# A decoder layer on one core: the first k tile for eight column groups in place of two k tiles for four, and six matmuls of a constant block around the norm factor

## The chip, the core and the metric

The kernel runs on one core of a Trainium2 chip. The core has engines that each work through their own list of instructions: TensorE (PE, matrix products; PEld is its loading of stationary operands), VectorE (DVE) and ScalarE (ACT) for elementwise work, GpSimd (POOL) and SyncE (SP), which here only issues loads. The engines run beside one another and wait for each other through semaphores. PE writes to an accumulation memory called PSUM; everything else lives in the on-chip memory SBUF, to which DMA brings the data.

The metric is the device time in microseconds. Before the change it is 1531.68 us, the median of three runs (1531.55 to 1531.72).

## What is computed

One decoder layer with 256 tokens of width 2048, in float32. Cut to what matters here:

```
mod = silu(c) W_ada + b_ada -> shift1, scale1, gate1, shift2, scale2, gate2
h   = RMSNorm(x)(1+scale1)+shift1
p   = h W_in, columns split into [retention q,k,v,g | HGRN2 q,f,i,g | branch gate A | branch gate B]
yA, yB = two attention-like branches on p, each with its own output product
x   = x + gate1 * ( (sigmoid(gA)*yA + sigmoid(gB)*yB) W_out )
h2  = RMSNorm(x)(1+scale2)+shift2
x   = x + gate2 * ( (silu(a) * b) W_down ),   [a, b] = split(conv3(h2 W_up))
out = RMSNorm_final(x)
```

The change touches the first half of the third line: 12 column groups of W_in, 512 columns each, that hold the q, f, i of the one branch and the q, k, v of the other (6144 of the columns).

## The kernel before

**Three products for one.** Each float32 factor is split into a high and a low half of a shorter type. A product is high x high, high x low and low x high. For a weight tile ACT makes the high half (line 165, tile `wh`), and DVE subtracts it from the raw tile to make the low half, here called the rest (line 170, `wl`). `load` (line 156) brings the raw tile by SP's queue; it has 12 buffers, `wh` and `wl` 4 each.

**Groups and k tiles.** The 2048 rows of W_in are 16 k tiles of 128. One k tile of one column group is 256 KB, and here called a unit: 192 units in all. For 8 of the 12 groups the result is kept transposed (`mm_cols`, lines 200 to 202: 12 matmuls a unit on 256 columns), for 4 (numbers 4, 5, 10 and 11) in rows (`mm_rows`, lines 187 to 189: 6 matmuls on 512).

**h arrives k tile by k tile.** For k tile k, scale and shift come from dot products over `w_ada`, which DVE takes in halves of 512 KB (`ada_dot`, line 389: four such halves for one k tile). ACT adds up the halves (lines 400, 401, 403) and makes the modulated tile's high half `hT` (line 336) and a full copy `h` (line 338 or 340); DVE makes its low half (line 341). So a k tile costs DVE four halves of about 1.1 us and a few small instructions, and a group can only go as far in k as h has come.

**The norm factor.** `token_rstd` sums the squares over the partitions by matmuls with a column of ones (line 289), ACT takes the root (line 298), DVE the reciprocal (line 299), and four matmul records with an identity (line 303) spread it over the partitions into PSUM as `rx`. `times` (line 379) multiplies x by it, and only then can hT for k tile 0 be made.

**Where sums are kept.** PSUM has two `pg` tiles of two banks each and four `po` tiles of one. Groups 0 and 1 (RESIDENT) keep their four `po` tiles from the first k tile to the last. Every other group is summed in a `pg` tile for as many k tiles as h has, and then leaves: at its first visit ACT copies the sum to SBUF (`take`, line 700), at later visits DVE adds it to what is there (line 702).

**The start.** FIRST = 4: for k tile 0 and then k tile 1, groups 0 to 3 run (lines 711 to 730). Groups 2 and 3 hold a `pg` tile each through both k tiles, and are copied out behind the loop (line 739). Everything up to line 733 that is marked with `pin` stays in program order on its engine; a scheduler places the rest at build time. The finished order of each engine is fixed in the program.

**The loop behind it.** From line 743 on `work` counts the units done. `have = min(KT, 2 + int((work - LAG) / ADA_EVERY))` with ADA_EVERY = 11 and LAG = 1 says how many k tiles of h there are to use. Groups are visited in turn 0 to 11, and each visit runs the group's k tiles up to `have` (two at a time in `pieces`). Between the pieces `pump` runs background generators by credit: the dot products of later k tiles, and the branches' work once their groups are complete. After these 192 units come the other products of the layer, in the same manner, up to the end.

Of the kernel before, what the change touches and what calls it, by code (L numbers as in the profile page):

```python
# [14 lines left out]
BF16 = mybir.dt.bfloat16  # L15
I32 = mybir.dt.int32
AF = mybir.ActivationFunctionType
ALU = mybir.AluOpType

P = 128  # L20
# [9 lines left out]
G = 512  # L30
NORM_EPS = 1e-6
HEAD_EPS = 1e-5
FIRST = 4
RESIDENT = 2
ADA_EVERY = 11
LAG = 1
NOSYNC = mybir.DependencyInfo(mybir.DependencyClass.NoSync, mybir.DependencyReason.DATA)
SMALL = 70

# [16 lines left out]
class Kernel:  # L56
# [172 lines left out]
    def constants(self):  # L229
        nc, a, c = self.nc, self.a, self.consts  # L230
        self.ones = c.tile([P, P], F32, name="ones")
        nc.vector.memset(self.ones, 1.0)
        self.eps1 = c.tile([P, 1], F32, name="eps1")
        nc.vector.memset(self.eps1, NORM_EPS)
        self.eps2 = c.tile([P, 1], F32, name="eps2")
        nc.vector.memset(self.eps2, HEAD_EPS)
        self.halfpi = c.tile([P, 1], F32, name="halfpi")
        nc.vector.memset(self.halfpi, math.pi / 2)

        self.silu = []  # L240
        self.sc = c.tile([P, D + 1], F32, name="sc")
        nc.vector.memset(self.sc[:, D:], 1.0)
        rows = [self.blk([1, GW], name="crow") for _ in range(2)]
        for u, row in enumerate(rows):
            nc.scalar.dma_start(out=row, in_=a["c"][:, u * GW : (u + 1) * GW])
        self.small_loads(nc.scalar, ("ident", "gn1"))
        for u in range(4):
            at = slice(u * G, (u + 1) * G)
            ps = self.po()
            nc.tensor.matmul(ps, lhsT=self.ones[0:1, :], rhs=rows[u // 2][:, u % 2 * G : (u % 2 + 1) * G], start=True, stop=True)  # L250
            self.silu.append((self.sc[:, at], ps))

    def small_loads(self, engine, names):
        for name in names:
            ap = self.a[name]
            t = self.consts.tile(list(ap.shape), ap.dtype, name=name)
            self.tc.keep_in_program_order(engine.dma_start(out=t, in_=ap))
            setattr(self, name, t)
# [22 lines left out]
    def token_rstd(self, parts):  # L281


        nc = self.nc
        ps = self.po()[:, :NT]
        for i, z in enumerate(parts):
            for t in range(NT):

                nc.tensor.matmul(
                    ps[:, t : t + 1],  # L290
                    lhsT=z[:, t * P : (t + 1) * P],
                    rhs=self.ones[:, 0:1],
                    start=i == t == 0,
                    stop=i == len(parts) - 1,
                    skip_group_check=True,
                )
        q = self.small([P, NT], name="rq")
        nc.scalar.activation(q, ps, AF.Sqrt, bias=self.eps1, scale=1.0 / D)
        self.pin(nc.vector.reciprocal(q, q))

        ps = self.po()[:, :T]
        for t in range(NT):
            nc.tensor.matmul(ps[:, t * P : (t + 1) * P], lhsT=q[:, t : t + 1].to_broadcast([P, P]), rhs=self.ident, start=True, stop=True)
        return ps

    def sqrt_table(self):
# [359 lines left out]
    def run(self):  # L666
        nc, a = self.nc, self.a
# [11 lines left out]
        def act(k):  # L679
            return hT[k // 2][:, k % 2, :]  # L680

        def ada1(k):
            if k > 0 and k % 2 == 0:
                ins = self.times(k, 2, rx_sb)
                self.tc.add_manual_dep(ins.ins, self.last.ins.name, NOSYNC, reason="behind the weights traced ahead of it")
            yield from self.scale_shift("ada1", k, s1, t1, self.gn1)
            if k % 2 == 0:
                hT[k // 2] = self.blk([P, 2, 2 * T], F32R, name="hT")
            self.modulated(act(k), self.xT[k // 4][:, k % 4, :], k, s1, t1)
            yield 0.7  # L690

        accs = [self.blk([P, NT, G] if c0 in ROWS else [P, 4, T], name="p") for c0 in ATT]
        done = [0] * len(ATT)
        mms = [self.mm_rows if c0 in ROWS else self.mm_cols for c0 in ATT]

        def take(g, ps, fresh):
            for at, z in self.parts(ps, ATT[g] in ROWS):
                dst = accs[g][:, at, :]
                if fresh:
                    nc.scalar.activation(dst, z, AF.Copy)  # L700
                else:
                    nc.vector.tensor_tensor(dst, dst, z, ALU.add)


        ada = [ada1(k) for k in range(KT)]
        for _ in range(3):
            next(ada[0])
        rx = self.token_rstd(parts)
        rx_sb = c.tile([P, T], F32, name="rx_sb")
        ps = [self.po2(), self.po2(), self.pg(), self.pg()][:FIRST]  # L710
        for k in range(2):
            for i in range(4 if k else 1):
                if k and i == 1:
                    self.times(k, 1, rx)
                next(ada[k])
            if k == 0:
                self.times(k, 1, rx)

            ahead = 2 * k
            uppers = [self.upper(a["wa"][g][:, k : k + 1, :], 1, G) for g in range(ahead + 1)]  # L720
            rests = [self.rest(z) for z in uppers[:ahead]]
            for _ in ada[k]:
                pass
            for g in range(FIRST):
                if g >= ahead:
                    rests.append(self.rest(uppers[g] if g < len(uppers) else self.upper(a["wa"][g][:, k : k + 1, :], 1, G)))
                wh, wl = rests[g]
                if k == g == 0:
                    self.pin(nc.scalar.activation(rx_sb, rx, AF.Copy))
                mms[g](ps[g], act(k), wh[:, 0, :], wl[:, 0, :], k == 0, k == 1 and g >= RESIDENT)  # L730
        for _ in range(2):
            next(ada[2])
        self.ordered = False
        for gen in ada[2:]:
            self.start(gen, 1)
        for g in range(FIRST):
            done[g] = 2
            if g >= RESIDENT:
                take(g, ps[g], True)
        self.pace(1, 4, ADA_EVERY / 2)  # L740
        self.pace(0, 3.5, 24)

        work = 2 * FIRST
        g = FIRST
        att, gates = [], []
        small = False
        while min(done) < KT:
            if work > SMALL and not small:
# [3 lines left out]
                self.start(self.lower_bound())  # L752
            have = min(KT, 2 + int((work - LAG) / ADA_EVERY))
            m = have - done[g]
# [18 lines left out]
            g = (g + 1) % len(ATT)  # L773
            if have == KT and done[0] < KT:
                g = min(i for i in range(len(ATT)) if done[i] < KT)
# [9 lines left out]
        for j in range(4):  # L785
            ps = self.rows(a["wb"][j], act)
# [55 lines left out]
        for j in range(4):  # L842
            last = j == 3
            x1.append(self.load_rows(j))
            g = self.row(self.gate["gate1"], j, "g1")
            ps = self.products(self.mm_rows, self.po2() if last else self.pg(), a["wout"][j], actm, 0, KT, hold=4 * last)
# [14 lines left out]
            if j == 2:  # L861
                part = self.row_part(ss)
# [232 lines left out]
```

## Time and profile before

| | before |
|---|---|
| median of 3 runs | 1531.68 us (1531.55 to 1531.72) |
| the profiled execution | 1532.02 us |
| its span, first to last instruction | 1529.9 us |
| PE busy | 1511.9 us, 99% |
| DVE busy | 1178.0 us, 77% |
| ACT busy | 841.5 us, 55% |
| 16 DMA engines, main queue | 76.1% |

The span is what the profile's rows cover; the execution's own time is 2.1 us more. Busy shares are means over the span. A row of the timeline gives start, duration, engine, source line, operation, output <- inputs, shape and count, and in brackets the idle time before and what ended it. `PE ... <- ACT hT L336` means that PE waited for line 336's result on ACT. A matmul's duration runs to the modelled end of its flow through the array, so the next starts before the last has ended: the space between starts, not the duration, is what a matmul costs PE.

### The profile page before, as it was taken

To read this page: it belongs to the slowest core of one execution; us is meant where nothing else is said; L and a number is where in the kernel's file an instruction comes from. 1 tells how busy PE (TensorE), PEld (TensorE's weight loads), DVE (VectorE), ACT (ScalarE), POOL (GpSimd) and SP (SyncE) were. 2 spreads that over 40 slices of the span, in tenths; PEclk is the share of its full clock that TensorE was granted. 3 is DMA by queue.
4 is the path that set the end of the run, shared out by engine and by line. 5 is a ranking of instruction groups with operands and counts; after the bars stand their busy time and mean duration, and the time that the engine had idled before them with its cause. 6 is when DMAs were issued, how large, how long until landed. Compare 5 with 4: busy or idle time off the path is not lost.

```text
span 1529.9 us, 22149 instructions
## 1 busy us (share of the span) xinstructions
PE 1511.9 (99%) x8258; PEld 1304.4 (85%) x8258; DVE 1178.0 (77%) x1610; ACT 841.5 (55%) x1194; POOL 4.0 (0%) x8
## 2 busy tenths in 40 slices
PE   8999999999999999999999999999999999999997
PEld 6999999888888888888878888888888888888886
DVE  7899996997998977898767777777777769455454
ACT  6655455766865554445456565555556558344343
POOL 0000000000000000000000000000000000000000
PEclk9999999999999999999999999999999999999999
DMA  9999996777777789989947777777777766676651
GB/s 375 370 355 328 311 332 217 240 278 239 274 240 264 256 293 323 323 300 341 336 126 231 231 235 233 237 227 232 232 231 232 227 191 192 204 209 206 194 166 55
DMA packets 110992, 385.68 MB, mean 252 GB/s; under 512 B 12802, under 2 KB 13346, under 8 KB 110884
## 3 DMA queue, kind: packets, MB, share of 16 engines
q1 hardware_dynamic: 110016, 383.14, 76.1%
q8 instruction: 64, 1.05, 0.3%
q10 hardware_dynamic: 868, 1.13, 0.2%
q14 instruction: 44, 0.36, 0.1%
HBM read 382.11 MB, written 2.11 MB: 251 GB/s over the span
## 4 chain that ended last, share of the span: by engine, by line
PE 95%; ACT 2%; DVE 1%; DMA 1%; issue 0%; SPq 0%; DVEq 0%; ACTq 0%
PE pg L187 13%; PE pg L188 13%; PE pg L189 13%; PE po L935 11%; PE pg L935 10%; PE po L937 5%; PE pg L937 5%; PE po L189 3%; PE po L187 3%; PE po L188 3%; PE pg L202 3%; PE pg L200 3%; PE pg L201 3%; PE po L565 1%; PE po L200 1%; PE po L201 1%
## 5 line engine op out<-in xcount | busy, mean ns | idle before, releaser
L170 DVE TENSOR_TENSOR wl<-raw,wh 128x1024 fp32r<-128x1024 f32 (+1 forms) x536 | 635.2, 1190 | 286.6 <-ACT wh L165 282.4
L165 ACT ACTIVATE wh<-raw 128x1024 fp32r<-128x1024 f32 (+1 forms) x536 | 551.1, 1033 | 544.1 <-PE pg L189 189.0
L389 DVE SCALAR_TENSOR_TENSOR raw<-raw,sc 128x1024 f32<-128x1024 f32 x192 | 233.5, 1219 | 0.0
L935 PE MATMUL pg<-h2T,wh 128*128 128x512 f32 x704 | 221.6, 396 | 0.6 <-ACT h L371 0.6
L935 PE MATMUL po<-h2T,wh 128*128 128x512 f32 x704 | 221.1, 395 | 0.0
L187 PE MATMUL pg<-wh,hT 128*128 128x512 f32 x512 | 202.7, 396 | 0.2 <-ACT p L700 0.2
L188 PE MATMUL pg<-wl,hT 128*128 128x512 f32 x512 | 200.1, 391 | 0.7 <-DVE wl L170 0.7
L189 PE MATMUL pg<-wh,hT 128*128 128x512 f32 x512 | 199.8, 390 | 0.0
L937 PEld LDWEIGHTS pg<-h2T,wl 128*128 128x128 f32 x704 | 132.1, 188 | 31.7 <-DVE wl L170 0.5
L937 PEld LDWEIGHTS po<-h2T,wl 128*128 128x128 f32 x704 | 132.2, 188 | 31.3
L937 PE MATMUL pg<-h2T,wl 128*128 128x256 f32 x704 | 138.5, 278 | 0.1
L937 PE MATMUL po<-h2T,wl 128*128 128x256 f32 x704 | 138.3, 278 | 0.0
L188 PEld LDWEIGHTS pg<-wl,hT 128*128 128x128 f32 x512 | 96.3, 188 | 21.0 <-DVE wl L170 2.2
L189 PEld LDWEIGHTS pg<-wh,hT 128*128 128x128 f32 x512 | 96.1, 188 | 20.3
L187 PEld LDWEIGHTS pg<-wh,hT 128*128 128x128 f32 x512 | 96.2, 188 | 19.4 <-ACT p L700 0.4
L202 PE MATMUL pg<-hT,wl 128*128 128x256 f32 x384 | 109.1, 284 | 0.6 <-DVE wl L170 0.6
L200 PE MATMUL pg<-hT,wh 128*128 128x256 f32 x384 | 109.2, 284 | 0.1
L201 PE MATMUL pg<-hT,wh 128*128 128x256 f32 x384 | 109.0, 284 | 0.0
L935 PEld LDWEIGHTS pg<-h2T,wh 128*128 128x128 f32 x704 | 107.2, 189 | 0.8 <-ACT h L371 0.8
L935 PEld LDWEIGHTS po<-h2T,wh 128*128 128x128 f32 x704 | 107.2, 189 | 0.0
L202 PEld LDWEIGHTS pg<-hT,wl 128*128 128x128 f32 x384 | 74.1, 193 | 0.8 <-DVE wl L170 0.8
L200 PEld LDWEIGHTS pg<-hT,wh 128*128 128x128 f32 x384 | 74.2, 193 | 0.6 <-ACT wh L165 0.2
(229 smaller groups left out, 2192.0 us busy)
## 6 DMA issues: line engine op xcount, KB each, us to landing
raw<-in_wup SPq DMA_DIRECT2D x176, 512.0 KB, 4.5
raw<-in_wdown SPq DMA_DIRECT2D x88, 512.0 KB, 4.3
raw<-in_wa SPq DMA_DIRECT2D x80, 512.0 KB, 5.7
raw<-in_ada SPq DMA_DIRECT2D x64, 512.5 KB, 5.7
raw<-in_ada SPq DMA_DIRECT2D x64, 512.0 KB, 5.8
raw<-in_wab SPq DMA_DIRECT2D x64, 512.0 KB, 5.0
raw<-in_gate SPq DMA_DIRECT2D x32, 512.5 KB, 4.7
raw<-in_wb SPq DMA_DIRECT2D x32, 512.0 KB, 5.2
```

What stands on the lines that cost most here:

```text
L165: self.pin(self.nc.scalar.activation(wh, raw, AF.Copy))
L170: self.last = self.nc.vector.tensor_tensor(wl, raw, wh.bitcast(F32), ALU.subtract)
L187: nc.tensor.matmul(ps[t], lhsT=hi, rhs=wh, start=first, stop=False)
L188: nc.tensor.matmul(ps[t], lhsT=hi, rhs=wl, start=False, stop=False)
L189: nc.tensor.matmul(ps[t], lhsT=lo, rhs=wh, start=False, stop=last)
L200: nc.tensor.matmul(out, lhsT=wh[:, cs], rhs=hi, start=opens, stop=False, skip_group_check=True)
L201: nc.tensor.matmul(out, lhsT=wh[:, cs], rhs=lo, start=False, stop=False, skip_group_check=True)
L202: nc.tensor.matmul(out, lhsT=wl[:, cs], rhs=hi, start=False, stop=last, skip_group_check=True)
L389: dot = self.pin(nc.vector.scalar_tensor_tensor(raw[:, 0, :], raw[:, 0, :], 1.0, self.sc[:, u * GW : u * GW + w], ALU.mult, ALU.mult, accu ...
L565: nc.tensor.matmul(ps[:, j * 64 : (j + 1) * 64], lhsT=(kt if n > 1 else k)[:, h, c * P : (c + 1) * P], rhs=eq[:, j * 64 : (j + 1) * 64], s ...
L935: self.pin(nc.tensor.matmul(ps[j + z], lhsT=wh[:, cs[z]], rhs=act, start=kt == 0, stop=False))
L937: nc.tensor.matmul(ps[j + z][:, :T], lhsT=wl[:, cs[z]], rhs=act[:, :T], start=False, stop=kt == KT - 1)
```

## The change

It has three parts.

1. FIRST becomes 8 and the start is written anew. Groups 0 to 7 run k tile 0 alone. Groups 0 and 1 stay in their `po` tiles; groups 2 to 7 each take a fresh `pg` tile for 12 (or 6) matmuls and are copied out by ACT at once (`take` inside the loop). The dot products of k tile 1 are spread between groups 3 to 6. Then groups 0 and 1 run k tile 1.
2. LAG becomes 7, and `work` starts from 10 units in place of 8.
3. `keep_busy(3)` puts three matmuls of a constant block (128 x 512, bf16, filled by POOL) on PE behind the sum of squares, and three more behind the spreading of the norm factor. They write to a `pg` tile that nobody reads. The matmuls of the norm factor are pinned now, so that this order holds.

```diff
-FIRST = 4
+FIRST = 8
-LAG = 1
+LAG = 7
...
+        self.busy = self.sb.tile([P, G], BF16, name="busy", tag="k1", bufs=7)
+        nc.gpsimd.memset(self.busy, 1.0)
+        self.spare = self.pg()[0]
...
+    def keep_busy(self, n):
+        for _ in range(n):
+            self.pin(self.nc.tensor.matmul(self.spare, lhsT=self.busy[:, :P], rhs=self.busy, start=True, stop=True))
...
+        self.keep_busy(3)
         q = self.small([P, NT], name="rq")
         nc.scalar.activation(q, ps, AF.Sqrt, bias=self.eps1, scale=1.0 / D)
         self.pin(nc.vector.reciprocal(q, q))
         ps = self.po()[:, :T]
         for t in range(NT):
...
+            self.pin(nc.tensor.matmul(ps[:, t * P : (t + 1) * P], lhsT=q[:, t : t + 1].to_broadcast([P, P]), rhs=self.ident, start=True, stop=True))
+        self.keep_busy(3)
         return ps
...
+        ps = [self.po2(), self.po2()]
+        def one(g, k):
+            return self.upper(a["wa"][g][:, k : k + 1, :], 1, G)
+        next(ada[0])
+        self.times(0, 1, rx)
+        part = one(0, 0)
+        for _ in ada[0]:
+            pass
+        for g in range(FIRST):
+            wh, wl = self.rest(one(g, 0) if g else part)
+            if g == 0:
+                self.pin(nc.scalar.activation(rx_sb, rx, AF.Copy))
+            to = ps[g] if g < RESIDENT else self.pg()
+            mms[g](to, act(0), wh[:, 0, :], wl[:, 0, :], True, g >= RESIDENT)
+            if g >= RESIDENT:
+                take(g, to, True)
+            done[g] = 1
+            if g >= FIRST - 5 and g < FIRST - 1:
+                next(ada[1])
+            if g == FIRST - 5:
+                self.times(1, 1, rx)
+        rests = [self.rest(one(g, 1)) for g in range(RESIDENT)]
+        for _ in ada[1]:
+            pass
+        for g in range(RESIDENT):
+            wh, wl = rests[g]
+            mms[g](ps[g], act(1), wh[:, 0, :], wl[:, 0, :], False, False)
+            done[g] = 2
...
-        for g in range(FIRST):
-            done[g] = 2
-            if g >= RESIDENT:
-                take(g, ps[g], True)
...
-        work = 2 * FIRST
+        work = FIRST + RESIDENT
```

The line numbers behind the new code grow: the copy of `take` is line 710 in place of 700, the addition 712 in place of 702, the dot halves 399 in place of 389.

ACT's list at the start, before, from the copy of the norm factor on. `wh` is a weight tile's high half, `pg` a finished group in PSUM, `p` its place in SBUF, `s`, `t`, `hT` and `h` belong to k tile 1:

```order
L729 ACTIVATE rx_sb<-po_166 128x256
L165 ACTIVATE wh_207<-raw_205 128x512
L165 ACTIVATE wh_225<-raw_223 128x512
L165 ACTIVATE wh_243<-raw_241 128x512
L400 ACTIVATE s_125<-dot_259 128x1
L401 ACTIVATE s_125<-gn_85,s_125 128x1
L165 ACTIVATE wh_278<-raw_276 128x512
L165 ACTIVATE wh_283<-raw_281 128x512
L165 ACTIVATE wh_288<-raw_286 128x512
```

ACT's list at the same place, now:

```order
L733 ACTIVATE rx_sb<-po_172 128x256
L165 ACTIVATE wh_214<-raw_212 128x512
L165 ACTIVATE wh_232<-raw_230 128x512
L710 ACTIVATE p_134<-pg_236 128x1024
L165 ACTIVATE wh_252<-raw_250 128x512
L710 ACTIVATE p_135<-pg_256 128x1024
L165 ACTIVATE wh_277<-raw_275 128x512
L710 ACTIVATE p_136<-pg_281 128x1024
L165 ACTIVATE wh_294<-raw_292 128x512
L710 ACTIVATE p_137<-pg_298 128x1024
```

Before, the high halves of groups 1 to 3 stood in one row and no copy of a sum lay between them (the first came behind seven more rows). Now the copy of group 2 stands ahead of the high half of group 3, the copy of group 3 ahead of the high half of group 4, and so on to group 7.

DVE's list around unit 28 of the 192, before. `wl` is a rest, `dot` a dot half, `p<-p,pg` an addition:

```order
L170 TENSOR_TENSOR wl_661<-raw_658,wh_660 128x1024
L379 TENSOR_TENSOR xT_96<-xT_96,rx_sb 128x512
L389 SCALAR_TENSOR_TENSOR raw_678,dot_677<-raw_678,sc 128x1024
L170 TENSOR_TENSOR wl_686<-raw_683,wh_685 128x1024
L170 TENSOR_TENSOR wl_704<-raw_701,wh_703 128x1024
L389 SCALAR_TENSOR_TENSOR raw_719,dot_677<-raw_719,sc 128x1025
L170 TENSOR_TENSOR wl_726<-raw_723,wh_725 128x1024
L389 SCALAR_TENSOR_TENSOR raw_756,dot_755<-raw_756,sc 128x1024
```

Its list around the same unit now:

```order
L170 TENSOR_TENSOR wl_660<-raw_657,wh_659 128x1024
L712 TENSOR_TENSOR p_134<-p_134,pg_563 128x1024
L399 SCALAR_TENSOR_TENSOR raw_675,dot_651<-raw_675,sc 128x1025
L712 TENSOR_TENSOR p_135<-p_135,pg_598 128x1024
L170 TENSOR_TENSOR wl_683<-raw_680,wh_682 128x1024
L351 TENSOR_TENSOR hT_517<-h_712,hT_517 128x256
L712 TENSOR_TENSOR p_136<-p_136,pg_630 128x1024
L170 TENSOR_TENSOR wl_720<-raw_717,wh_719 128x1024
```

Where there were rests and dot halves only, additions now stand among them. Over the whole program the additions are 54 in place of 37. The rests of 1024 columns are 498 in place of 504 and those of 512 columns 44 in place of 32, and the high halves and loads likewise.

More of the change, by code (lines that the diff above doesn't have):

```diff
@@ L287, in token_rstd @@
             for t in range(NT):
-                nc.tensor.matmul(
+                self.pin(nc.tensor.matmul(
                     ps[:, t : t + 1],
@@ L295, in token_rstd @@
                     skip_group_check=True,
-                )
+                ))
+        self.keep_busy(3)
         q = self.small([P, NT], name="rq")
@@ L302, in token_rstd @@
         for t in range(NT):
-            nc.tensor.matmul(ps[:, t * P : (t + 1) * P], lhsT=q[:, t : t + 1].to_broadcast([P, P]), rhs=self.ident, start=True, stop=True)
+            self.pin(nc.tensor.matmul(ps[:, t * P : (t + 1) * P], lhsT=q[:, t : t + 1].to_broadcast([P, P]), rhs=self.ident, start=True, stop=True))
+        self.keep_busy(3)
         return ps
@@ L709, in run @@
         rx_sb = c.tile([P, T], F32, name="rx_sb")
[L710 to L723, printed above, removed]
-            for g in range(FIRST):
[L725 to L730, printed above, removed]
+        ps = [self.po2(), self.po2()]
[26 more added lines that the diff above has]
+            done[g] = 2
         for _ in range(2):
@@ L735, in run @@
             self.start(gen, 1)
-        for g in range(FIRST):
-            done[g] = 2
-            if g >= RESIDENT:
-                take(g, ps[g], True)
         self.pace(1, 4, ADA_EVERY / 2)
         self.pace(0, 3.5, 24)
-        work = 2 * FIRST
+        work = FIRST + RESIDENT
         g = FIRST
```

## The prediction

> **What bounds the kernel now.** I read the page's totals and the chain that ended last first, then who made TensorE (PE) wait, then the first 40 us in order of time on PE, ScalarE (ACT) and VectorE (DVE), then stretches of the span.
>
> ```profile
> span 1529.9 us, 22149 instructions
> PE 1511.9 (99%) x8258; PEld 1304.4 (85%) x8258; DVE 1178.0 (77%) x1610; ACT 841.5 (55%) x1194; POOL 4.0 (0%) x8
> ...
> PE 95%; ACT 2%; DVE 1%; DMA 1%; issue 0%; SPq 0%; DVEq 0%; ACTq 0%
> ```
>
> PE is the bound: 95% of the last chain is its own. Time that PE loses is lost for good, and it can only be given back where PE waits. The list of PE's waits shows how little that is (waiter, what it waited for: us, times, longest).
>
> ```profile
> PE po L200 <- ACT hT L336: 1.7, 2, 1.2
> PE po L303 <- DVE rq L299: 1.4, 1, 1.4
> ...
> PE pg L202 <- DVE wl L170: 0.6, 1, 0.6
> ...
> PE po L201 <- DVE hT L341: 0.2, 1, 0.2
> PE pg L187 <- ACT p L700: 0.2, 1, 0.2
> ```
>
> These five, 4.1 us, all lie in the first 40 us, and so does the change. PE in order of time there (start, us, shape, count, idle time before):
>
> ```profile
> 14.41 1.22 PE L303 MATMUL po<-ident,rq 128*128 128x128 f32 x4 [1.37 <-DVE rq L299]
> 16.82 0.79 PE L200 MATMUL po<-hT,wh 128*128 128x256 f32 x2 [1.19 <-ACT hT L336]
> ...
> 22.36 0.41 PE L201 MATMUL pg<-hT,wh 128*128 128x256 f32 x1
> 22.57 0.36 PE L202 MATMUL pg<-hT,wl 128*128 128x256 f32 x1
> 22.77 0.28 PE L200 MATMUL pg<-hT,wh 128*128 128x256 f32 x1
> 22.89 0.28 PE L201 MATMUL pg<-hT,wh 128*128 128x256 f32 x1
> ...
> 35.00 0.39 PE L188 MATMUL pg<-wl,hT 128*128 128x512 f32 x1
> 35.23 0.39 PE L189 MATMUL pg<-wh,hT 128*128 128x512 f32 x1
> ...
> 38.29 0.28 PE L201 MATMUL pg<-hT,wh 128*128 128x256 f32 x1
> 39.12 0.39 PE L202 MATMUL pg<-hT,wl 128*128 128x256 f32 x1 [0.55 <-DVE wl L170]
> 39.34 0.28 PE L200 MATMUL pg<-hT,wh 128*128 128x256 f32 x1
> ```
>
> Starts are 0.21 us apart up to 22.57 and 0.12 from 22.77 on, for the same matmul: PE runs slow until 22.6 us, 5.8 us after its dense run began at 16.82. I call one k tile of one group a unit: 12 matmuls at 0.12, 1.44 us, or for the four row groups 6 at 0.227 (35.00 to 35.23), 1.36 us. From 16.82 to 39.12 PE does 8 units of the one kind, 4 of the other and two matmuls, 17.2 us of work in 22.3. **It loses 5.1 us**: about 2.5 to the slow clock (27 matmuls x 0.093), the rest to waits. That is all the change can win behind 16.82. The two gaps ahead of that (1.37 and 1.19) end with the norm factor and hT, which the change does not make earlier.
>
> **What the change costs at the start.** In the new order of ACT the copy of each finished group out of PSUM (line 710, 700 before) stands in front of the next group's high half (line 165). ACT works strictly in order, so from group 3 on: group ends, copy, high half, rest on DVE, next group's matmuls. PE has nothing else behind the waiting matmul but six of group 1. The old kernel shows this sequence once, in the chain that ended last:
>
> ```profile
> 35.66 1.03 ACT p L700
> 36.86 0.96 ACT wh L165
> 37.84 1.24 DVE wl L170
> 39.12 0.39 PE pg L202
> ```
>
> There it cost PE just the 0.55, since another group's matmuls lay in between. The prices of the steps, from the rows of ACT and DVE:
>
> ```profile
> 22.29 0.29 ACT L400 ACTIVATE s<-dot 128x1 f32<-128x1 f32 x1 [3.69 <-DVE raw L389]
> ...
> 22.91 1.24 ACT L165 ACTIVATE wh<-raw 128x512 fp32r<-128x512 f32 x2
> 24.40 0.63 ACT L165 ACTIVATE wh<-raw 128x512 fp32r<-128x512 f32 x1 [0.26 <-PE po L201]
> 24.94 0.28 ACT L403 ACTIVATE t<-dot 128x1 f32<-128x1 f32 x1
> 25.25 0.60 ACT L336 ACTIVATE hT<-xT,t,s 128x256 fp32r<-128x256 f32 x1
> 25.76 0.58 ACT L340 ACTIVATE h<-xT,t,s 128x256 f32<-128x256 f32 x1
> ...
> 36.58 0.28 ACT L403 ACTIVATE t<-dot 128x1 f32<-128x1 f32 x1
> 36.76 1.05 ACT L165 ACTIVATE wh<-raw 128x1024 fp32r<-128x1024 f32 x1
> ```
> ```profile
> 26.38 0.43 DVE L341 TENSOR_TENSOR hT<-h,hT 128x256 fp32r<-128x256 f32 x1 [0.62 <-ACT h L340]
> ...
> 110.76 0.69 DVE L170 TENSOR_TENSOR wl<-raw,wh 128x512 fp32r<-128x512 f32 x1
> ```
>
> From one group's end to the next group's: the copy starts 0.04 after the last matmul's end (35.23 + 0.39 to 35.66); the next ACT instruction starts 0.92 later (36.58); high half 0.63; 0.03 to DVE (36.76 + 1.05 to 37.84); rest 0.69; 0.04 to PE (37.84 + 1.24 to 39.12): the first matmul on a rest starts 2.35 behind the old group's end. Two matmuls on high halves ran meanwhile; 0.22 and eight spaces of 0.12 later the twelfth starts, which takes 0.28: **3.8 us a group instead of 1.44**, and for row groups 2.35 + 4 x 0.23 + 0.39, 3.7 instead of 1.36. There are five rounds, to the ends of groups 3 to 7 (4 and 5 are row groups), and one holds two small scale instructions too (22.29 to 22.91, 0.62): 3.8 + 3.7 + 3.7 + 4.4 + 3.8 = 19.4.
>
> Behind group 7 come the copy 0.96, two high halves (0.54 each, 24.40 to 24.94), t 0.18, a 1024-wide half 0.95, hT 0.51, h 0.58 and, on DVE, hT's low half 0.43, with small gaps **4.9 us until PE is dense**, nine matmuls on their way. From group 2's end that is 24.3 us with 8.8 of work (groups 3 to 7, 7.04; six and nine matmuls, 1.8): 15.5 lost.
>
> Ahead of group 2's end lie 30 matmuls from 16.82. The six constant ones fit the gaps: 512 columns at the slow clock are 0.227 x 0.213/0.12, 0.40, three are 1.2, and the gaps are 1.37 and 1.19. Bounds: 0, or 0.3 if each load of weights adds a tenth; I take 0. Their use is the clock. The dense run begins near 13.0 now (14.41 less 1.37); with the 5.8 us seen above, speed comes at 18.8, so 9 matmuls are slow, and 18 of the old 27 save 0.093 each, 1.7 us (bounds 0 and 2.5). Group 2 ends at 16.82 + 9 x 0.21 + 21 x 0.12 + 0.16, 21.4, 1.0 lost. In sum 16.5 lost against 5.1: **+11.4 us.**
>
> The Trainium skill (TensorE: Matmul & The Clock Gate, Part 1) has PE at half clock by default and at full speed after one window of about 3.4 us of sustained work. The slow and fast spacing agrees with it. By its figure the clock could rise from 16.4 us on, and my sum would be some 0.8 smaller.
>
> **What it costs later.** LAG 7 and one k tile in place of two split the rest into more and smaller visits of a group, and each visit of groups 2 to 11 after its first ends with an addition on DVE. They number 37 now (first row below, from the groups by line between 16 and 300 us); by the loop's arithmetic they become 54, early above all: through unit 60 of 192, 16 for 7.
>
> ```profile
> L702 DVE TENSOR_TENSOR p<-p,pg 128x1024 f32<-128x1024 f32 x37 | 45.0, 1217 | 9.2 <-PE pg L202 7.2 <-PE pg L189 1.8
> ...
> 106.21 1.22 DVE L170 TENSOR_TENSOR wl<-raw,wh 128x1024 fp32r<-128x1024 f32 x1
> 107.35 1.21 DVE L702 TENSOR_TENSOR p<-p,pg 128x1024 f32<-128x1024 f32 x1
> 108.48 1.22 DVE L170 TENSOR_TENSOR wl<-raw,wh 128x1024 fp32r<-128x1024 f32 x1
> ...
> 80.00:160.00 80.00, 80.00 (x551) 74.67 (x550) 78.59 (x111) 42.15 (x62) 0.95 (x1) 1.00 0.97 336
> ```
>
> The last row is a stretch: PE 80.00 busy, DVE 78.59 of 80 (third sum). DVE has no room there. An addition, a 1024-wide rest or half a dot product takes 1.14 of its queue (106.21, 107.35, 108.48), a 512-wide rest 0.60. Between units 20 and 100 DVE had 45 rests, 14 additions, 29 dot halves and 25 small ones: 104.3 us for 80 units, which are 113.1 of PE. Now it has 47, 28, 28 and 20: **118.3 us, 5 more than PE needs**. DVE would enter that stretch some 3.6 ahead (PE, dense at 45.7 with 8.75 units done, is at unit 20 at 60.2; DVE has a dozen instructions from there to that unit's rest, near 56.6), so at least 1.7 of PE waiting; at most the 14 extra additions in full, 16. Additions also hold the queue until their group ends, so the lead is never used whole. Walked row by row with these prices, the new order gives waits of 0.2 to 0.7 at a dozen places between 110 and 180 us and near the last groups, **5 us** in all. I take 5.
>
> ```profile
> raw<-in_wa SPq DMA_DIRECT2D x80, 512.0 KB, 5.7
> ```
>
> At nothing: SP's loads, whose order in the new start alternates dot halves and weights. One lands 5.7 us after its issue (row), twelve buffers are ahead, and a round of 3.8 uses one or two. They cost only if PE ran faster than now. Then six more loads and wh halves (12 of 512 columns for 6 of 1024), since ACT is busy 42.15 of 80 in that row; they cost if ACT were near 80. The fill of the constant block on POOL, 4.0 us busy in the whole span, has 10 us until PE reads it. The spare PSUM tile is free before group 3 wants it. The profiled execution took 1532.02, the span and 2.1 around it, 0.34 over the median of 1531.68. 1532.02 + 11.4 + 5 = 1548.4; as a median **1548 us**.
>
> **Rivals.**
>
> *Rounds alone* (22%): DVE's lead absorbs the additions. For it: PE did not wait on DVE once from 80 to 160. Against it: no spare time there. 1531.7 + 11.4 = 1543.
>
> *The additions in full* (10%): DVE falls behind at once and the 16 go to PE: 1531.7 + 11.4 + 16 = 1559. Against it: a lead exists.
>
> *The clock falls again in the rounds* (10%), where PE works about 1.4 of 3.8 us:
>
> ```profile
> 1515.00:1530.00 15.00, 6.52 (x29) 5.07 (x27) 7.04 (x14) 3.49 (x8) 0.00 (x0) 0.82 0.38 140
> ```
>
> The clock was 0.82 over these 15 us; at half speed that is 5.4 us, from 1524.6, 3 us after PE's work ended at 1521.5. The rounds' gaps are about 2. If they sufficed, ten matmuls a round would take 0.093 longer, 5 rounds, 5 us: 1553. The same page of the Trainium skill says that one idle window of about 3.4 us brings half speed back, which speaks against this rival.
>
> *Not slower* (7%): the copies leave PE free, as where PE has another group's matmuls to hand. Then of the 5.1 lost some 2.6 come back and DVE's 5 stay out: 1529. It decides as soon as a group's high half is ready before its predecessor's copy; against it stands ACT's order, copy first.
>
> **Numbers.** Forecast 45%, 1548; rivals as given; 6% unnamed. Its own range is 1545 to 1551. To leave out no more than 2 in 10, 1541 to 1556 takes in the rounds alone with the fullest gain of the clock and the cold rounds. A change counts as seen from 0.2%, 3.1 us. Faster 0.04, within 0.2% 0.03, slower 0.93.
>
> **What would show it.** Right: between 21 and 46 us five PE waits near 2 us on line 165 or 170, copies of line 710 each followed by one high half; 0.12 spacing before 20 us; then waits of PE for rests between 110 and 180. Wrong: a dense PE before 40 us (the rounds fall), no waits behind 100 us (rounds alone), matmuls 0.21 apart behind 23 us (cold rounds).

## The result

The changed kernel takes 1555.53 us, the median of five runs (1553.95 to 1556.37), against 1531.68 us of five runs of the kernel before (1531.55 to 1532.06). The ratio is 1.0155, with a 95% interval of 1.0141 to 1.0168: 23.9 us slower. The prediction had 1548, a range of 1541 to 1556 and 0.93 for slower. Direction and range held, and the cost was half as much again as the 16.3 us forecast.

The page of the profile after: the span, PE's granted clock in 40 slices, and the groups of PE that wait most (busy, mean ns of one, idle time before them and what ended it).

```profile
span 1554.5 us, 22218 instructions
PEclk8899999999999999999999999999999999999999
L187 PE MATMUL pg<-wh,hT 128*128 128x512 f32 x512 | 204.9, 401 | 3.9 <-ACT wh L165 3.8
L188 PE MATMUL pg<-wl,hT 128*128 128x512 f32 x512 | 202.0, 395 | 0.8 <-DVE wl L170 0.8
L200 PE MATMUL pg<-hT,wh 128*128 128x256 f32 x384 | 110.0, 287 | 8.8 <-ACT wh L165 8.8
L202 PE MATMUL pg<-hT,wl 128*128 128x256 f32 x384 | 110.7, 289 | 2.4 <-DVE wl L170 2.2
```

PE now waits for high halves (8.8 and 3.8 us) and for rests (2.2 and 0.8). These waits add up to 15.6, and 24.6 us of span have to be explained. To see where they lie I lined up the two traces from the back: for a given amount of PE work still to do (matmuls left, each at its full-speed spacing), how much later does the changed kernel reach that point than the one before? The lateness is 16.4 us at 59 us of the old kernel, 20.2 at 351, 24.9 at 431, and from there it stays to the end (24.75). So there are three losses: **16.4 at the start, 3.8 between 60 and 350 us, 4.6 near 400 us.** The forecast had 11.4, 5 and nothing.

**The start.** The rounds are there, in the order forecast. ACT and PE in one of them (start, us, idle time before):

```profile
29.82 1.02 ACT L710 ACTIVATE p<-pg 128x1024 f32<-128x1024 f32 x1 [3.32 <-PE pg L189]
30.74 0.62 ACT L165 ACTIVATE wh<-raw 128x512 fp32r<-128x512 f32 x1
...
34.68 1.02 ACT L710 ACTIVATE p<-pg 128x1024 f32<-128x1024 f32 x1 [3.32 <-PE pg L189]
```
```profile
31.41 0.80 PE L187 MATMUL pg<-wh,hT 128*128 128x512 f32 x1 [1.63 <-ACT wh L165]
```

The copy waits for PE's group, the high half stands behind the copy, PE waits 1.63 for it, and at 34.68 the next copy starts: 4.86 us for one round, where the forecast had 3.7 to 4.4. The matmuls of such a round stand 0.21 apart, which the prediction named as the sign of a cold clock:

```profile
42.99 0.41 PE L200 MATMUL pg<-hT,wh 128*128 128x256 f32 x1
43.20 0.41 PE L201 MATMUL pg<-hT,wh 128*128 128x256 f32 x1
```

The granted clock agrees (stretch: length, busy time and count of PE, PEld, DVE, ACT, POOL, then the clock, DMA share, GB/s):

```profile
17.80:24.50 6.70, 4.84 (x38) 4.44 (x38) 2.97 (x6) 1.69 (x3) 0.00 (x0) 1.00 1.03 401
24.60:34.80 10.20, 8.36 (x20) 4.94 (x19) 3.88 (x7) 3.21 (x5) 0.00 (x0) 0.50 0.84 318
34.90:38.20 3.30, 1.10 (x7) 0.90 (x8) 1.34 (x2) 1.89 (x4) 0.00 (x0) 1.00 0.52 187
38.30:51.80 13.50, 8.59 (x37) 7.77 (x36) 6.45 (x11) 6.66 (x10) 0.00 (x0) 0.50 0.61 185
```

Full speed came at 17.8 us, as early as forecast (18.8). It was gone at 24.6, after one round, and except for 3.4 us it stayed away until 51.9. One round ran at full speed, 21.06 to 24.96 by the starts of the copies, 3.9 us. The other four took 4.86, 4.86, 4.97 and 4.86.

**Between 60 and 350 us** DVE has no time left. The same stretch of 80 us that the prediction showed with 78.59 of DVE and 80.00 of PE now reads:

```profile
80.00:160.00 80.00, 78.75 (x540) 72.91 (x540) 79.67 (x101) 38.88 (x57) 0.96 (x1) 1.00 0.89 297
```

PE stands idle for 1.25 of these 80 us. The cost is more than that, since the modelled end of a matmul covers the first 0.16 us of each wait: from 80 to 175 us the spaces between starts are 3.6 us longer in sum than at full speed. Nearly all of it lies at 0.1 to 0.8 us a time before or just behind a matmul of line 202, which takes a rest, the last of this stretch at 168 us. PE's waits from 50 to 330 us:

```profile
PE pg L202 <- DVE wl L170: 1.8, 4, 0.6
```

**Near 400 us** stands what the forecast did not have. ACT and PE in order of time, in the product behind the 192 units, whose last additions lie near 317 us:

```profile
386.50 1.06 ACT L165 ACTIVATE wh<-raw 128x1024 fp32r<-128x1024 f32 x1 [3.50 <-PE pg L189]
...
395.20 1.28 ACT L272 ACT_TABLE_LOAD   x1
...
396.69 1.08 ACT L502 ACTIVATE f<-f,lb,lb 128x256 f32<-128x256 f32 x2
397.79 1.28 ACT L805 ACT_TABLE_LOAD   x1
399.09 1.03 ACT L805 ACTIVATE gt<-pg 128x1024 f32<-128x1024 f32 x1
400.01 1.14 ACT L505 ACTIVATE k<-f,ones 128x1024 f32<-128x1024 f32 x1
401.05 1.05 ACT L165 ACTIVATE wh<-raw 128x1024 fp32r<-128x1024 f32 x1
```
```profile
402.14 0.50 PE L187 MATMUL pg<-wh,hT 128*128 128x512 f32 x1 [2.16 <-ACT wh L165]
403.40 0.77 PE L188 MATMUL pg<-wl,hT 128*128 128x512 f32 x1 [0.76 <-DVE wl L170]
403.97 0.63 PE L189 MATMUL pg<-wh,hT 128*128 128x512 f32 x1
404.39 0.63 PE L187 MATMUL pg<-wh,hT 128*128 128x512 f32 x1
```

The high half at 401.05 is the first since 386.50. Of the 13.5 us between the two ACT was busy for 13.3 with squares, table loads and gates, nearly all of a branch (the count in the expectations below, 10.3, is too low). PE ran out of halves, waited 2.16 and 0.76, and then ran at half speed (0.43 a matmul of 512 columns, not 0.23) until 406.9. That is 2.9 + 1.7 = 4.6. In the kernel before, the same work lies between the high halves at 368.95 and 383.27 us, with one more in the middle, so its longest stretch without one has 9.1 us of ACT's work, and PE waited only 0.2 there:

```profile
373.02 1.04 ACT L165 ACTIVATE wh<-raw 128x1024 fp32r<-128x1024 f32 x1
...
383.27 1.05 ACT L165 ACTIVATE wh<-raw 128x1024 fp32r<-128x1024 f32 x1
```

### The profile page after: what moved, and what is told of

It is laid out like the page before. It is cut to its first block, busy times and chain, and to the rows that moved or that the text cites. A ratio compares the mean times of both kernels' runs of the same rounds, so it can differ in the third digit from the quotient of the medians.

```text
span 1554.5 us, 22218 instructions
## 1 busy us (share of the span) xinstructions
PE 1525.4 (98%) x8264; PEld 1309.6 (84%) x8264; DVE 1197.2 (77%) x1633; ACT 846.8 (54%) x1201; POOL 4.6 (0%) x9
## 4 chain that ended last, share of the span: by engine, by line
PE 91%; DVE 5%; ACT 2%; issue 1%; DMA 1%; DVEq 0%; ACTq 0%
PE pg L187 13%; PE pg L188 13%; PE pg L189 13%; PE po L951 11%; PE pg L951 10%; PE po L953 5%; PE pg L953 5%; PE po L187 3%; PE po L189 3%; PE po L188 3%; PE pg L202 2%; PE pg L200 2%; PE pg L201 2%; DVE wl L170 2%; DVE raw L399 1%; PE po L575 1%
## 5 line engine op out<-in xcount | busy, mean ns | idle before, releaser
L187 PEld LDWEIGHTS pg<-wh,hT 128*128 128x128 f32 x512 | 97.1, 190 | 24.9 <-ACT wh L165 5.3
L200 PEld LDWEIGHTS pg<-hT,wh 128*128 128x128 f32 x384 | 74.5, 194 | 10.6 <-ACT wh L165 10.3
```

Of the source, the lines that this page charges most:

```text
L187: nc.tensor.matmul(ps[t], lhsT=hi, rhs=wh, start=first, stop=False)
L200: nc.tensor.matmul(out, lhsT=wh[:, cs], rhs=hi, start=opens, stop=False, skip_group_check=True)
```

## The experiments

The theory after the result was: ACT's order makes the rounds; the cold clock makes them longer; the additions make the middle; ACT's order near 400 us, which the lag moved, makes the last part. The rivals were that the smaller pieces themselves or DVE cost the time at the start too, that the clock costs nothing, and that the part near 400 us follows from the start or the additions. All times stand beside runs of the kernel before on the same chip, which read 1532.5 to 1532.9 in the three comparisons, 1 us above the first; ratios are safer than differences from 1531.68. The lateness "at the start" comes from one profile of each kernel, and part of it has nothing to do with the edits: PE's first dense matmul (the first on an hT) stands at 16.82 us before and at 16.69 in the changed kernel, but between 16.69 and 18.49 in the profiles of kernels whose code is the same up to there (column of the table below). In 123, for one, DVE waited 2.5 us for ACT's squares of x from 8 to 14 us, in the changed kernel 0.3.

**ahead.** In the loop over groups, pinned as the rest of the start:

```
-            wh, wl = self.rest(one(g, 0) if g else part)
+            wh, wl = self.rest(part)
...
+            if g + 1 < FIRST:
+                part = one(g + 1, 0)
             if g >= RESIDENT:
                 take(g, to, True)
```

> The changed kernel with one step moved: the next group's high half is made ahead of the copy that empties the last group, so ACT no longer has both between two groups. Serial rounds (what the prediction says): the five rounds, 23.4 us from group 2's end at 21.02 to group 7's at 44.46, fall to about 1.6 to 1.8 a group, the longer of PE's 1.44 and ACT's copy and half of 1.55; that is 15 us less, and with the clock up again by then 2 more: 1539 to 1541, or up to 1543 if DVE then waits more. Rival, the time goes for the smaller pieces and more additions themselves: 1555. The shift near 400 us stays in both.

Measured: 1544.60 us (1543.81 to 1546.62), ratio 1.0080 (1.0067 to 1.0092). The loss at the start fell from 16.4 to 4.4. The middle (4.2) and the part near 400 us (4.7) stayed. The five rounds took 10.4 us (22.37 to 32.74 by the copies' starts) in place of 23.5. So ACT's order is what made the rounds, and the smaller pieces did not. It is about 3 us above the expectation: the rounds took 10.4 us where 8 to 9 stood, and one wait and one cold stretch were left behind group 7 (waits of PE from 16 to 60 us, then the clock):

```profile
PE po L200 <- ACT hT L346: 3.0, 1, 3.0
PE pg L200 <- ACT wh L165: 0.5, 1, 0.5
```
```profile
36.80:40.20 3.40, 3.40 (x17) 3.40 (x18) 3.40 (x6) 1.88 (x5) 0.00 (x0) 0.50 1.02 366
```

**warm.** More constant matmuls in the gaps, with waits and ACT's order as they are:

```
+            if g > RESIDENT:
+                self.keep_busy(6, to[0])
             mms[g](to, act(0), wh[:, 0, :], wl[:, 0, :], True, g >= RESIDENT)
...
+        self.keep_busy(12, self.pg()[0])
         rests = [self.rest(one(g, 1)) for g in range(RESIDENT)]
```

> The changed kernel with more constant matmuls, six ahead of each of groups 3 to 7 in their own PSUM tile and twelve behind group 7: PE's gaps are filled, its waits and ACT's order stay. Cold clock: the granted clock stays full from 17.8 us on through the rounds, four rounds of 4.9 become 3.9 and the 4.1 us at half speed from 47.75 become 2.1: about 6 us less, 1549.5. Rival, the rounds are ACT's alone and the clock costs nothing: 1555.5, or up to 1558 where the fill stands ahead of a ready group.

Measured: 1553.28 us (1553.17 to 1555.16), ratio 1.0138 (1.0122 to 1.0153). The clock in the rounds:

```profile
20.00:50.00 30.00, 26.43 (x152) 17.63 (x151) 14.64 (x24) 15.23 (x22) 0.00 (x0) 1.00 0.82 285
```

It stayed full for the whole start, the five rounds took 19.6 us in place of 23.5 (22.22 to 41.80 by the copies' starts), and the loss at the start fell to 12.6. So with a warm clock the start costs about what the prediction summed for it without its gain of the clock (11.4 + 1.7 = 13.1), and the cold clock cost **3.8 us** on top, not the 6 of the expectation. By the end the gain is 2.9, since the half speed near 400 us lasted 6.8 us in this profile and not 3.4. The 3.8 rests on one profile of each kernel: the intervals of the ratios, 1.0138 and 1.0155, overlap. Two more profiles bear it out: in those of *nobusy* and 123 (below) full speed outlasted three rounds, and the five took 20.7 and 20.8 us.

**busy_only and nobusy.** The six constant matmuls added to the kernel before, and taken out of the changed one:

```
-        self.keep_busy(3)
...
-        self.keep_busy(3)
```

> The kernel before with the six constant matmuls alone. The prediction's clock term: full speed 4 to 5 us earlier, 18 matmuls that save 0.093 each, 1.7 us (bounds 0 and 2.5), and the constant matmuls themselves cost nothing: 1530.0, or 1531.0 where the day's time of before is 1.0 longer, as in the last comparison. Rival: the start's gaps pull the clock down again, or the waits of the start and not PE's speed set the time there: no change, 1531.7 to 1532.7.

Measured: 1533.01 us (1532.08 to 1533.72, 11 runs), ratio 1.0001 (0.9992 to 1.0010): no change. A gain of 1.7 us would be 0.9989, outside the interval. PE waits 1.3 for hT behind its first groups, and half speed came back behind that wait:

```profile
PE po L200 <- ACT hT L346: 1.3, 1, 1.3
```
```profile
27.80:31.00 3.20, 3.20 (x17) 3.20 (x16) 3.20 (x6) 1.06 (x1) 0.00 (x0) 0.50 1.03 414
```

A faster PE there only comes to the next wait earlier, or loses the speed again.

> The changed kernel without the six constant matmuls. The prediction's term alone: 1.7 us more, 1557.2. Windows of 3.4 us that must be nearly full for the clock to rise: none is full before the rounds end, so groups 0 to 2 run at half speed throughout and all five rounds are of 4.9 us: 2.7 more, 1558, and no full speed in the record before 50 us. If the clock does not set the start: 1555.5.

Measured: 1556.90 us (1556.01 to 1559.01), ratio 1.0160 (1.0146 to 1.0174), which can't be told from 1.0155. My expectation of a record without full speed was wrong: it came at 21.9 and lasted 17 us through three rounds, then half speed for 13.7. The loss at the start was 16.5, as with the constant matmuls. So in the kernel before they gain nothing like 1.7, and in the changed one neither a cost nor a gain of that size can be told from the spread. What they do to the clock can be seen: counted from PE's first dense matmul, full speed came between 0.9 us ahead of it and 4.1 behind in the ten profiles with them, and 4.2 to 5.9 behind in the three without.

**b_lag7.** The kernel before with `LAG = 7`, nothing else.

> The kernel before with the lag of 7 alone: its start is as it was, but the visits become smaller and the additions on DVE 50 in place of 37 (the changed kernel has 54). The prediction priced 17 more at 5 us, the changed trace shows 3.8 between 80 and 300 us: for 13 more that is 3 to 4 us. ACT's order near 400 us has the same stretch of 10.3 us as the changed kernel: if that makes the shift there, 4.6 more. Together 1539; without the shift 1535; if the additions hide behind DVE's lead here and only the start made them cost, 1536 with the shift and 1532 without.

Measured: 1541.98 us (1540.23 to 1543.03), ratio 1.0058 (1.0045 to 1.0070), 9.3 us. The lateness is 0.7 at 59 us, 4.4 at 351 and 9.0 at 431. So the lag alone makes both later losses: 3.7 in the middle and 4.6 near 400 us. The waits of the middle (50 to 330 us) are for rests and additions of DVE, but also 1.2 for an hT: about 2.4 of the 3.7 stand at one place near 128 us, where PE waited for that hT and then for a rest, with DVE busy for 39.70 of the 40 us up to 130. Those near 400 us (380 to 430) are the same as in the changed kernel:

```profile
PE pg L187 <- ACT hT L336: 1.2, 1, 1.2
PE pg L188 <- DVE wl L170: 0.8, 1, 0.8
PE pg L187 <- DVE p L702: 0.6, 1, 0.6
PE pg L200 <- DVE p L702: 0.3, 1, 0.3
```
```profile
PE pg L187 <- ACT wh L165: 2.2, 1, 2.2
PE pg L188 <- DVE wl L170: 0.8, 1, 0.8
```

**lag1.** The changed kernel with `LAG = 1`.

> The changed kernel with the lag back at 1: its start is the same, the additions on DVE are 40 in place of 54 (the kernel before has 37). If the additions make the shift of 3.8 us between 80 and 300 us, in proportion to their number, it falls to about 1: 1552.7. If the start makes it (eight groups at one k tile, later vectors), it stays: 1555.5. ACT's order near 400 us has the long stretch as in the changed kernel, so 4.6 us there stay.

Measured: 1555.09 us (1553.52 to 1556.46), ratio 1.0146 (1.0132 to 1.0160). The sum hardly moved, but its parts did. The additions (from 16 to 330 us) are 40, and the middle no longer loses anything (-0.4 in place of 3.8). The start lost 19.9 in this profile, which is of the slowest of the four runs. Of the 3.5 more, 1.8 lie ahead of the first dense matmul, which the lag does not touch. Another 1.3 us is a wait near 58 us for a copy to empty its PSUM tile (waits from 50 us on); what brought that wait there was not tried. The clock was at half speed for 27 us. Near 400 us nothing was won: the loss is 5.5, with the same wait of 2.2 for a high half and the same stretch of 13.3 us of ACT's other work. So the new start brings that order without the lag, as the lag brings it without the new start.

```profile
L712 DVE TENSOR_TENSOR p<-p,pg 128x1024 f32<-128x1024 f32 x40 | 48.5, 1214 | 1.3 <-PE pg L189 1.1
```
```profile
PE pg L200 <- ACT wh L165: 3.3, 1, 3.3
PE pg L187 <- ACT p L710: 1.3, 1, 1.3
```
```profile
26.10:53.30 27.20, 18.23 (x61) 13.92 (x60) 11.13 (x21) 11.85 (x18) 0.00 (x0) 0.50 0.65 211
```

So the lag is the middle's cause, from both sides, and not the only cause of the part near 400 us. That it acts through DVE's additions rests on DVE's full stretch and on what PE waited for, not on a run with the additions alone.

**p123 and p114.** The number that paces the branches' work over these products:

```
-        self.pace(0, 122.0, 88)
+        self.pace(0, 123.0, 88)
```

(and 114 in the other).

> The changed kernel with one number of the background's pace from 400 us or so set to 123 in place of 122. By the durations of the trace this cuts the longest stretch of other work that ACT does between two high halves near 400 us from 10.3 us to 6.4. If that stretch is what makes the shift of 4.6 us there (a wait of 2.2 and 0.8 and then 3.4 us at half speed), it goes: 1551. If the shift comes from the additions or from the start, it stays: 1555.5.

> The changed kernel with the background's pace number at 114 in place of 122. Counting ACT's work near 400 us from its order and the trace's durations, against 2.72 us of PE work for each high half, ACT falls behind by at most 7.2 us in the kernel before, 9.6 in the changed one, 7.4 with 123 (where 2.8 of the 4.6 us were left) and 7.0 with 114. If this backlog against PE's stock of ready halves makes the shift near 400 us, it is gone or under 1 us: 1551 to 1552. If not, 1555.5.

Measured: with 123, 1555.21 us (1553.71 to 1555.44), ratio 1.0145 (1.0131 to 1.0158), and a loss near 400 us of 2.5 in place of 4.6: the waits became shorter and the clock stayed full. With 114, 1553.66 us (1552.17 to 1554.23), ratio 1.0135 (1.0121 to 1.0149), and a loss of 0.1. The waits there (380 to 430 us), of 123 and of 114:

```profile
PE pg L188 <- DVE wl L170: 1.8, 3, 0.9
```
```profile
PE pg L188 <- DVE wl L170: 0.2, 1, 0.2
```

Cutting the longest stretch of other work alone (123, 6.8 us of ACT's work) was not enough; the count of ACT's whole backlog was the better guide, though no exact one: with 112, whose count is the lowest (6.0), the last three kernels below, which have other lags, lose 1.5 there. So the loss comes with the place of the branches' work in ACT's list, which the pace number moved while the code of the start and the number of additions stayed as they were. With 114 another 1.0 is lost near 500 us, and this profile's start lost 17.7 (the 1.3 more than in the changed kernel lie ahead of the first dense matmul), so only part of the 4.6 shows in the time, and the intervals of its ratio and of 1.0155 overlap.

**undo3, ready2, ready3.** The three causes undone together (*ahead*, `LAG = 1`, pace 112), and two attempts at a version that beats both kernels: the second k tile's activations and halves two groups earlier, with a lag of 2 and of 3.

```
+            if g == FIRST - 2:
+                for _ in ada[1]:
+                    pass
+            if g == FIRST - 1:
+                parts = [one(g, 1) for g in range(RESIDENT)]
             if g >= RESIDENT:
                 take(g, to, True)
...
-            if g >= FIRST - 5 and g < FIRST - 1:
+            if g >= FIRST - 6 and g < FIRST - 2:
                 next(ada[1])
```

> The changed kernel with its three suspected costs undone together: the next group's high half ahead of the copy, the lag at 1, the background's pace number at 112 (ACT's greatest backlog near 400 us by the count of the last expectations: 6.0 us, 9.6 in the changed kernel). If the account is complete, what is left over before is the 4.4 us that the first of these left at the start, up to 1.5 for the wait near 58 us that the lag of 1 alone showed, and up to 1 for other places that the pace shifted: 1537 to 1540 where before takes 1532.8. If the three are not additive or a cause is missing: above 1542.

> As the last one, with a lag of 2, and the second k tile's activations and its halves for the two resident groups made two groups earlier, ahead of the last copies. The wait of 3.1 us behind group 7 and the 3.4 us at half speed that came with it (1.7) should go: of the 4.4 us left at the start about nothing remains. Additions 41 (before: 37), so 0 to 1 for them: 1532 to 1534, beside 1532.8 of before. If the wait only moves (ACT or DVE short of time later, as in the wait near 58 us), 1535 to 1537.

> The same with a lag of 3: 45 additions, 22 of them before unit 100 (before: 16, the changed kernel 30), so about 1.5 us for them by proportion, and the third k tile's vectors are wanted a unit later, so no wait near 58 us: 1533 to 1535. Whichever of the two lags is faster tells what the lag buys (vectors later) against what it costs (more additions).

Measured: 1536.84 us, ratio 1.0029 (1.0018 to 1.0039); 1536.12, 1.0023 (1.0014 to 1.0032); 1536.79, 1.0027 (1.0016 to 1.0038). The first leaves 4.8 of 24.75 us in its profile and 4.3 in the medians, at the low end of the 4.2 to 7.2 expected: the account has no large part missing. In the second the wait for hT is gone and the clock stayed full, but DVE came too late with rests (waits from 20 to 330 us):

```profile
PE pg L202 <- DVE wl L170: 3.3, 4, 1.5
PE pg L188 <- DVE wl L170: 0.8, 3, 0.4
```

So the wait moved from ACT to DVE, as that expectation's second branch had it. The third missed its 1533 to 1535; its profile has the same waits. Between the lags of 2 and 3 no difference can be told. No version here beats the kernel before.

All profiles in one table: lateness against the kernel before, in us, by place (places by the old kernel's time; each from one profiled execution). The column to 59 us takes in what the first dense matmul came later.

| kernel | first dense matmul at (16.82 before) | to 59 us | 59 to 351 | 351 to 431 | behind | sum |
|---|---|---|---|---|---|---|
| changed | 16.69 | 16.4 | 3.8 | 4.6 | -0.1 | 24.75 |
| ahead | 17.46 | 4.4 | 4.2 | 4.7 | -0.2 | 13.1 |
| warm | 17.35 | 12.6 | 3.9 | 5.5 | -0.1 | 21.8 |
| nobusy | 17.68 | 16.5 | 3.8 | 4.6 | 0 | 24.9 |
| lag1 | 18.49 | 19.9 | -0.4 | 5.5 | -0.1 | 24.85 |
| p123 | 18.46 | 17.2 | 3.8 | 2.5 | 0.3 | 23.85 |
| p114 | 18.05 | 17.7 | 3.9 | 0.1 | 1.0 | 22.65 |
| b_lag7 | 18.01 | 0.7 | 3.7 | 4.6 | -0.1 | 8.9 |
| busy_only | 17.63 | 1.5 | 0 | 0 | 0 | 1.5 |
| undo3 | 17.16 | 4.0 | -0.3 | 1.5 | -0.4 | 4.8 |
| ready2 | 17.64 | 2.8 | -0.4 | 1.5 | -0.3 | 3.6 |
| ready3 | 17.65 | 1.9 | 1.4 | 1.5 | -0.4 | 4.45 |

## Why the prediction was right and where it was wrong

- **The rounds: right.** Copy ahead of half ahead of rest, five times, each with a wait of PE on line 165 or 170. The one round at full speed took 3.9 us, forecast 3.8, and the five took 19.6 in *warm*, forecast 19.4. *ahead* shows it by taking the order away: 12.0 us less at the start, cold rounds included.
- **The clock in the rounds: wrong.** "The clock falls again in the rounds" stood as a rival with 10% and 5 us. It happened, on top of the forecast and not in place of it, and the profile of *warm* prices it at 3.8 at the start. The step that failed is the argument against it: half speed 3 us behind the end of PE's work at 1521.5 was read as needing 3 us of idleness, and a page of the Trainium skill (TensorE: Matmul & The Clock Gate, Part 1) was called in support. The traces show that less is enough: here a stretch of 3.41 us with 1.71 without a matmul (last section).
- **The clock's gain: wrong.** The 1.7 us for an earlier full speed did not come, neither alone (*busy_only*, 1.0001) nor so that it could be told within the change (*nobusy*, 1.0160 to 1.0155). The speed came as early as forecast, but PE then only met the next wait earlier. With the two terms of the clock put right the start adds up: 12.6 (*warm*) for a forecast of 13.1 without the gain, and 3.8: 16.4.
- **The constant matmuls at no cost: right as far as it can be told.** *busy_only* is not slower (at most 1.5 us by the interval). That PE's first dense matmul came at 16.69 us and not later than the 16.82 before shows little, since the same code put it at 18.49 in another profile.
- **The additions: right in kind, a little too dear.** 5 forecast, 3.8 measured; DVE full in the stretch named, waits of 0.2 to 0.8 from 115 to 168 us, about where they were named. *b_lag7* and *lag1* show the lag as its source from both sides; the additions as the way it acts are argued.
- **The part near 400 us: missing.** The prediction followed the lag to DVE's additions and stopped there, and put ACT behind the start at nothing. But the lag (*b_lag7*, 4.6) and the new start (*lag1*, 5.5) each move when the groups end, and with that the place of the branches' work in ACT's list against high halves. The prediction had the mean of ACT's load, 42.15 of 80 us, which says nothing of a stretch of 13.3 without a high half; it read ACT's new list only at the start.
- **The rivals.** *Rounds alone* falls (the additions do cost), *additions in full* falls (3.8, not 16), *not slower* falls.

In sum: 11.4 + 5 forecast; 16.4 + 3.8 + 4.6 measured. That the range held is in part luck. Its upper end of 1556 had room for cold rounds but for nothing near 400 us, and without that part the time would be about 1551; with it the median lies 0.5 below the end, and two of the five runs lie above it.

## What to carry to other kernels

When a start is cut into pieces, write down each engine's list in its new order and look for a producer's next piece that stands behind a consumer's clean-up of the last one: that makes a serial round out of an overlap, and here it cost more than everything else. A number that spaces the work (a lag, a pace) moves all that is placed relative to it, so the whole program is to be searched for stretches in which an engine's other work exceeds the stock of ready tiles. Short waits of PE that come in every round counted twice here, because they also took the clock away; add up the idle time of such a stretch and do not judge each gap by itself.

## What the runs showed of the hardware

In all thirteen traces each stretch of full or half speed between two changes of the clock lasts a multiple of 3.41 us (3.4, 6.8, 10.2, 13.7, 17.1, 27.3 among the short ones), on a grid that starts elsewhere in each execution. The Trainium skill (TensorE: Matmul & The Clock Gate, Part 1) describes such free-running windows of 3413 ns, and the traces agree. It also says that half speed comes back after at least one idle window. Here the traces differ, and the measurement decides: by the matmul records (whose ends are modelled) 27 of the 28 periods at full speed with more than 1.65 us without a matmul were followed by half speed. The one that was not (114, from 807.8 us) had 1.80, the least idle that was had 1.52, and others kept full speed with up to 1.63. So a period of 3.41 us that is about half idle is mostly enough, with a divide between 1.5 and 1.8 that idle time alone does not settle. In *warm* no period of the start had more than 1.2, and full speed stayed. Full speed came back only behind a period with at most 0.4 us idle, and not behind each such.

That fits how differently the same start came out. A round of 3.8 or 3.9 us at full speed has up to 1.9 idle, and the periods in such rounds hold 0.7 to 1.9, at times right at the divide. With 123 (same code at the start) full speed outlasted three rounds, with PE busy for 9.96 of 17.00 us, and then fell:

```profile
22.60:39.60 17.00, 9.96 (x54) 7.19 (x54) 7.68 (x13) 6.73 (x10) 0.00 (x0) 1.00 0.81 290
39.70:53.20 13.50, 8.59 (x37) 7.77 (x37) 7.06 (x11) 7.40 (x11) 0.00 (x0) 0.50 0.64 195
```

A round at half speed has 1.63 idle in 4.86 us, so hardly any period is full, and the clock mostly stays down. Five runs of the changed kernel spread by 2.4 us (mean clock 0.990 to 0.993, the fastest run with 0.993), those of the kernel before by 0.5, but by 1.4 to 2.3 in the three later comparisons, which have 9 to 19 runs of it. So the grid's place may make part of this spread; the runs do not show it. In the profiles of *nobusy* and 123 the rounds took 2.7 us less than in the changed kernel, but there full speed came only 4 us behind the first dense matmul (1.1 in the changed one), so that counted from that matmul the start was just 0.9 cheaper.
